# Unit 1's gelu moved ahead of unit 2's second centre tap, and half of the gate and residual of rows 0 to 3 moved into stage P3 of the down product

## The chip, the cores and the metric

The kernel runs on one core of one Trainium2 chip. A core has five engines that run their own instruction streams side by side: TensorE (PE in the profile; PEld is its weight load), VectorE (DVE), ScalarE (ACT), GpSimd (POOL) and SyncE (SP, which here only issues DMAs). Each stream runs in its written order, and an instruction that waits for another engine holds up everything behind it in its own stream. The metric is the time of one execution on the device in microseconds (us), lower is better.

## The reference

One block of a diffusion transformer on 1024 tokens of 1024 channels: token mixers, a layer norm, a feed-forward part with a 3x3 depthwise convolution, and a last layer norm. The change touches the feed-forward part and the last layer norm alone:

```
def conv_ffn(h, w_up, conv_w, conv_b, w_down, grid_rows):
    a, g = jnp.split(h @ w_up, 2, axis=-1)
    bsz, t, f = a.shape
    a = dwconv3x3(a.reshape(bsz, grid_rows, t // grid_rows, f), conv_w).reshape(bsz, t, f) + conv_b
    return (jax.nn.gelu(a, approximate=False) * g) @ w_down

# in reference(), with ALPHA = 2 ** 0.25 and mx[5] the gate of the second half
        ffn_x = conv_ffn(modulate(x_new, mx[3], mx[4]), ffn_up[l], ffn_conv_w[l], ffn_conv_b[l], ffn_down[l], rows)
        x_new = layer_norm(ALPHA * x_new + mx[5] * ffn_x, ln2_g[l], ln2_b[l])
```

All of it is computed in float32; the kernel splits each operand of a product into a high and a low part and multiplies three times.

## The kernel before

All engine calls go through one helper, so nearly every instruction carries line 57 in the profile, and groups are told apart by their tiles.

**The up product.** `ffn_up` works through 22 units of 128 hidden channels. Each unit is one Strassen-like product of seven partial products, numbered 1 to 7 in the code (a step such as "(3,2)" below is unit 3, product 2), of twelve 128x512 matmuls each. The convolved half of a unit collects in a pair of PSUM banks, `zv` (tile psA), of which there are two, so that unit 3's pair is the one that unit 1 gives back when its gelu has read it. The other half goes through single banks (tile psB). A unit's vector work is: `a` is formed on DVE for the two halves of the tokens, `centre(g, a)` puts the centre tap and bias into `zv` on ACT (tile psA from a, par), `conv` adds the other eight taps on DVE (eight SCALAR_TENSOR_TENSOR into psA), `gelu` reads `zv` on ACT into tile `h`, and `finish` multiplies `h` by the gate half on DVE. Weight halves are cut by `prepare(n)`: ACT casts the high part (tile wf), POOL subtracts to get the low part.

The first three units are started by hand (`u0`, `u1`, `u2` in `ffn_up`), with every engine's order written out; from unit 3 on a loop does the same in a fixed rhythm. In the hand-written part, `u1.conv()` runs on DVE while PE does (2,3), (1,4), (2,4) and (3,1). Then DVE forms u2's second `a`, ACT does u2's second centre tap, and DVE does `u1.finish` and `u2.conv()`. (3,2) opens unit 3's pair of banks; (3,3) adds to that pair's second bank, after ACT has copied `r` out of it and, on the pair's first bank, done unit 3's first centre tap.

**The down product.** `ffn_down` is one more such product of 1024x2816 by 2816x1024, of seven stages in the order 1, 2, 6, 5, 3, 7, 4 (called P1 and so on), with 11 forms (hidden slices) in each and 4 row tiles of 12 matmuls in all for each form. Accumulators X (stages 1, 6, 7, 4) and Y (2, 5, 3) are four PSUM banks each, one for each row tile of a half; the first two are tile psB, the others psA. Form i+4's high part is cast on ACT (`high`) and its low part subtracted on DVE (`low`, two instructions of 128x512 a form in P7 and P4: tiles fl and dw) at the start of iteration i. In stages 5, 7 and 4 the last 3, 3 and 5 forms are multiplied at the end, row tile by row tile, so that some row tiles are done earlier.

Outputs are eight row tiles (tile fy) of two column halves. Rows 0 to 3 get their first half from P1 and P2, their second half from P1, P6 (copied out of X at the start of P5) and P5, P3 (in Y). `out(t, c, bank, add)` gives the steps for row t, half c: `begin` adds the bank, `mid` fetches the residual input over the POOL queue (tile fx, three buffers) and multiplies by the gate row, `end` adds ALPHA times the residual and takes `bn_stats` of the half. `chain` makes mean and inverse deviation from those statistics, `last(t, c)` does the two layer-norm instructions on a half and sends it out. These steps stand in a list `todo`, from which each iteration takes one (two in the first five of P7) after its `low`, so they share DVE's one queue with the low parts that PE waits for. Rows 4 to 7 end with X after P7 (second half: `begin`, which must read X before P4 may add to it) and after P4 (first half), the latter as the program's tail: rows 6 and 7 first, then 4, then 5, each with its own `chain` and `last`.

Of the kernel before, what the change touches and what calls it, by code (L numbers as in the profile page):

```python
# [7 lines left out]
F32 = mybir.dt.float32  # L8
# [4 lines left out]
ALU = mybir.AluOpType  # L13
# [3 lines left out]
P = 128  # L17
T = 1024
D = 1024
# [6 lines left out]
ALPHA = 2.0 ** 0.25  # L26
# [41 lines left out]
class Builder:  # L68
# [1034 lines left out]
    def ffn_up(self, ys):  # L1103

        nc = self.nc
        tt = nc.vector.tensor_tensor
        us = [self.Unit(self, f) for f in range(FT)]
        u0, u1, u2 = us[:3]
        w11, w12, a0, g0 = self.first
        last = FT - 1  # L1110
# [96 lines left out]
        def go(u, k):  # L1207
            assert self.plan[self.at] == (u.f, k)
            bank = {6: u.x, 5: u.v, 7: u.x, 3: u.v, 4: u.x}[k]
            self.product(k, bank, self.forms.pop((u.f, k)), k == 5)  # L1210
            self.at += 1
# [41 lines left out]
        u1.conv()  # L1253
        go(u2, 3)
        tt(out=u2.a[:, 1], in0=u2.v, in1=u2.s[:, 1], op=ALU.add)
        u2.centre(1, u2.a[:, 1])
        self.prepare(self.at + 5)
        go(u1, 4)
        self.prepare(self.at + 5)
        u1.gelu()  # L1260
        go(u2, 4)
        self.prepare(self.at + 5)
        u1.finish((u1.x, u1.r[1]))
# [3 lines left out]
        for f in range(3, FT):  # L1267
# [8 lines left out]
            while self.at < len(self.plan) and self.plan[self.at][0] == f:  # L1276
                k = self.plan[self.at][1]
# [3 lines left out]
                if k == 7 and 4 <= f < 12:  # L1281
                    j = 36 + f
                    nc.vector.tensor_tensor_reduce(out=ada, in0=ada, in1=silc, scale=1.0, scalar=self.par[:, C_ADAB + j:C_ADAB + j + 1],
                                                   op0=ALU.mult, op1=ALU.add, accum_out=self.mods[:, j:j + 1])
# [157 lines left out]
    def ffn_down(self, dn):  # L1442
        nc, HF = self.nc, self.HF
        tt = nc.vector.tensor_tensor
# [24 lines left out]
        def load(i):  # L1469
            k, f = plan[i]  # L1470
            if k == 1 and f == 8:
                stores()
            if k == 1 and i < 3:
                return
            r = raws[i] = raw()
            h = {1: (0, 0), 2: (0, 1), 3: (0, 1), 4: (1, 1)}.get(k)
            src = self.h_part(*h, f) if h else self.s3[f][:, :] if k == 7 else self.s12[f][:, 1 if k == 6 else 0]
            nc.sync.dma_start(r[:, 0], src)
            if k == 1:
                nc.sync.dma_start(t1[f], self.w_part(0, 0, f))  # L1480
            w = {2: (1, 0), 3: (1, 1)}.get(k)
            if w:
                nc.sync.dma_start(r[:, 1], self.w_part(*w, f))
            if k == 3:
                exs[i] = self.Rt(nm="s2")
                nc.sync.dma_start(exs[i], self.s12[f][:, 1])

        def extra():
            return dn.tile([P, 2, 512], F32, tag="ex", bufs=3, name=self.name("ex"))
# [62 lines left out]
        ys, st = {}, {}  # L1552
        half = (slice(0, 512), slice(512, D))

        def new_y(t):
            if t not in ys:
                ys[t] = dn.tile([P, D], F32, tag="fy", bufs=8, name=self.name("fy"))
                st[t] = self.small([2, 6], nm="bnd", bufs=8)
            return ys[t]

        def out(t, c, bank, add):

            x, y = {}, new_y(t)[:, half[c]]

            def fetch():
                x[0] = dn.tile([P, 512], F32, tag="fx", bufs=3, name=self.name("fx"))
                nc.gpsimd.dma_start(x[0], self.xnew[t][:, half[c]])

            def begin():
                if add:  # L1570
                    tt(out=y, in0=y, in1=bank, op=ALU.add)
                else:
                    fetch()
                    tt(out=y, in0=bank, in1=gate[:, half[c]], op=ALU.mult)

            def mid():
                fetch()
                tt(out=y, in0=y, in1=gate[:, half[c]], op=ALU.mult)

            def end():  # L1580
                self.residual(x[0], y, st[t][:, c, :])
            if add:
                return begin, mid, end
            return begin, end
# [15 lines left out]

        def last(t, c):
            m, r = stat[t]
            y, s = ys[t][:, half[c]], half[c]
            nc.vector.scalar_tensor_tensor(out=y, in0=y, scalar=m, in1=lng[:, s], op0=ALU.subtract, op1=ALU.mult)
            nc.vector.scalar_tensor_tensor(out=y, in0=y, scalar=r, in1=lnb[:, s], op0=ALU.mult, op1=ALU.add)
            (nc.gpsimd if t < 4 else nc.sync).dma_start(self.out[t * P:(t + 1) * P, s], y)

        def both(*parts):
            def run():
                for p in parts:  # L1610
                    p()
            return run

        todo = []
        for i in range(LD):
            load(i)
        gate, lng, lnb = rows = [dn.tile([P, D], F32, name=n) for n in ("gate5", "ln2_g", "ln2_b")]
# [5 lines left out]
        for i in range(N):  # L1623
            k, f = plan[i]
            if i + LD < N:
                load(i + LD)
            if i < 3:

                nc.sync.dma_start(t1[i], self.w_part(0, 0, i))
            if i == 18:  # L1630
                nc.sync.dma_start(gate, self.gate5.broadcast_to([P, D]))
            if i in (20, 22):
                self.row(("ln2_g", "ln2_b")[(i - 20) // 2], rows[(i - 18) // 2])
            for l, _, at, by in sums:
                j = i - at + 3
                if j >= 0 and j % by == 0 and j // by < HF:
                    l(j // by)
            if i + LP + 1 < N:
                high(i + LP + 1)
            if i + LP < N:  # L1640
                low(i + LP)
            if i == 0:
                u = self.prev
                u.new = lambda shape, nm: extra()
                u.gelu()
                u.fetch()
                u.finish()
                for part in u.sums():
                    part()
            for _, g, at, by in sums:  # L1650
                j = i - at
                if j >= 0 and j % by == 0 and j // by < HF:
                    g(j // by)
            if i == first[2]:
                Y = [self.bank("B"), self.bank("B")]
                yp = self.pair()
                Y += [yp[:, 0], yp[:, 1]]
            n = group.get(k, 0)
            if f < HF - n:
                for t in range(4):  # L1660
                    multiply(i, t)
            elif f == HF - 1:
                if k == 4:
                    for g in todo:
                        g()
                    todo = []

                for part in ((2, 3), (0,), (1,)):
                    for t in part:
                        for j in range(i - n + 1, i + 1):  # L1670
                            multiply(j, t)
                    for t in part:
                        if k == 5:
                            nc.scalar.copy(new_y(4 + t)[:, half[1]], Y[t])
                        elif k == 7:
                            b, *e = out(4 + t, 1, X[t], True)
                            b()
                            todo += e
                        else:
                            for g in out(4 + t, 0, X[t], False):  # L1680
                                g()
                    if k == 4:
                        chain(*(4 + t for t in part))
                        for t in part:
                            for c in range(2):
                                last(4 + t, c)

            if f < 4:
                if k == 2:
                    nc.scalar.copy(new_y(f)[:, half[0]], X[f])  # L1690
                elif k == 5:
                    nc.scalar.copy(ys[f][:, half[1]], X[f])
            if f == 0 and k == 5:
                for x in zip(mids, ends):
                    todo += x
            if f == 0 and k in (6, 7):
                o = [out(t, 0 if k == 6 else 1, Y[t], True) for t in range(4)]
                todo += [x[0] for x in o]
                mids, ends = [x[1] for x in o], [x[2] for x in o]
                if k == 7:  # L1700
                    fin = [lambda t=t, c=c: last(t, c) for t in range(4) for c in range(2)]
                    todo += [mids[0], both(ends[0], mids[1]), both(ends[1], mids[2]), both(ends[2], mids[3]), both(ends[3]),
                             both(lambda: chain(0, 1, 2, 3), fin[0]), *fin[1:]]
            for _ in range(2 if k == 7 and f < 5 else 1):
                if todo:
                    todo.pop(0)()
# [47 lines left out]
```

## Time and profile before

| what | value |
|---|---|
| time, median of 3 runs | 1317.91 us (1316.45 to 1319.5) |
| the profiled execution's own time | 1315.14 us |
| its span, first to last instruction | 1313.4 us |
| mean granted TensorE clock | 0.99 |
| DVE busy | 1015.4 us |
| ACT busy | 550.9 us |
| POOL busy | 363.4 us |
| HBM read, written | 168.32 MB, 39.08 MB |

A profile row in order of time gives start, duration, engine, line, operation, output tile from input tiles, shape and count; a bracket at its end is the idle time of that engine just before, with the tile that released it. Start-to-start distances are shorter than durations where an engine overlaps one instruction's end with the next one's start. A row by stretch gives, for the stretch, its length, busy time and instructions of PE, PEld, DVE, ACT and POOL, then the granted TensorE clock (1.00 is full), the DMA share and GB/s. The seven stages of the down product follow each other from 1077 us; P3 stands at about 1198 to 1228 us, P7 at 1228 to 1258, P4 from 1261, and DVE works alone from where PE ends.

### The profile page before, as it was taken

The numbers are of one execution on the slowest core, as the hardware profiler recorded it, in microseconds if no ns is written. First come the engines' busy times: TensorE is split into PE (matmuls) and PEld (weight loads), VectorE is DVE, ScalarE is ACT, GpSimd is POOL, SyncE is SP. The second block draws the span as 40 slices with busy tenths as digits, with TensorE's granted clock in tenths as the row PEclk, the third lists the DMA queues.
The fourth block names the chain that finished last, engine by engine and source line by source line (L and its number), as shares of the span: only waits on it lengthen the run. The fifth ranks groups of instructions, "written<-read, shape, count | busy, mean of one in ns | idle before, by whom it ended". The sixth has DMA issues, their size and how long they took to land. (4 is left out here: it accounts for less than half of the span.)

```text
span 1313.4 us, 17643 instructions
## 1 busy us (share of the span) xinstructions
PE 1244.1 (95%) x6348; PEld 1044.6 (80%) x6348; DVE 1015.4 (77%) x1790; ACT 550.9 (42%) x980; POOL 363.4 (28%) x309
## 2 busy tenths in 40 slices
PE   4999999999999989999998999999999999999993
PEld 3887888889888878777876788888888888888872
DVE  7968984686949768697797777777766776988797
ACT  4836444443332241345363444444344443545420
POOL 0000000000000000000017788888988872000020
PEclk9999999999999999999999999999999999999997
DMA  9763234104123054346564434542443268999242
GB/s 332 265 198 124 96 121 152 49 24 159 54 71 113 17 178 144 124 167 206 172 188 135 172 117 159 177 136 89 160 145 124 101 228 306 352 312 363 88 145 89
DMA packets 99672, 208.56 MB, mean 159 GB/s; under 512 B 10224, under 2 KB 31360, under 8 KB 99584
## 3 DMA queue, kind: packets, MB, share of 16 engines
q1 hardware_dynamic: 94784, 190.65, 42.7%
q0 software_dynamic: 4800, 16.78, 3.5%
q8 instruction: 50, 0.82, 0.2%
q14 instruction: 38, 0.31, 0.1%
HBM read 168.32 MB, written 39.08 MB: 158 GB/s over the span
## 5 line engine op out<-in xcount | busy, mean ns | idle before, releaser
L57 DVE SCALAR_TENSOR_TENSOR psA<-a,par,psA 128x945 f32<-128x945 f32 (+2 forms) x176 | 215.9, 1227 | 21.6 <-ACT psA L57 16.2
L57 PE MATMUL psA<-x,wf 128*128 128x512 f32 x708 | 172.2, 392 | 6.4 <-ACT h L57 3.4
L57 PE MATMUL psB<-xk,wf 128*128 128x512 f32 x672 | 176.7, 390 | 0.9 <-ACT s L57 0.9
L57 PEld LDWEIGHTS psA<-x,wf 128*128 128x128 f32 x708 | 133.8, 189 | 35.8 <-ACT psA L57 3.9
L57 PEld LDWEIGHTS psB<-xk,wf 128*128 128x128 f32 x672 | 126.1, 188 | 27.7 <-ACT s L57 1.3
L57 POOL DMA_DIRECT2D wd<-pk x16 | 8.7, 542 | 500.7 <-ACT pk L57 463.0
L57 PE MATMUL psA<-xh,wh 128*128 128x512 f32 x320 | 126.8, 396 | 2.0 <-ACT wh L57 1.2
L57 POOL TENSOR_TENSOR wf<-raw,wf 128x512 fp32r<-128x512 f32 x95 | 123.1, 1301 | 20.0 <-ACT wf L57 19.4
L57 PE MATMUL psA<-xh,wl 128*128 128x512 f32 x320 | 126.1, 394 | 0.1
L57 PE MATMUL psA<-xl,wh 128*128 128x512 f32 x320 | 125.9, 393 | 0.0
L57 PE MATMUL psB<-x,wf 128*128 128x512 f32 x384 | 104.7, 389 | 0.0
L57 PEld LDWEIGHTS psB<-x,wf 128*128 128x128 f32 x384 | 72.0, 188 | 15.3 <-issue 0.2
L57 ACT CAST wh<-r 128x512 fp32r<-128x512 f32 x76 | 44.5, 619 | 84.7 <-PE psA L57 57.3
L57 ACT CAST wf<-raw 128x512 fp32r<-128x512 f32 x95 | 58.7, 618 | 47.5 <-PE psA L57 27.4
L57 DVE TENSOR_TENSOR a<-psA,s 128x512 f32<-128x512 f32 x39 | 27.0, 691 | 60.6 <-PE psA L57 59.0
L57 PEld LDWEIGHTS psA<-xh,wh 128*128 128x128 f32 x320 | 60.2, 188 | 14.1 <-ACT wh L57 1.6
L57 PEld LDWEIGHTS psA<-xh,wl 128*128 128x128 f32 x320 | 60.2, 188 | 12.4 <-DVE wl L57 0.5
L57 PEld LDWEIGHTS psA<-xl,wh 128*128 128x128 f32 x320 | 60.2, 188 | 11.7 <-issue 0.2
L57 DVE TENSOR_TENSOR kq<-kq,F 128x1024 f32<-128x1024 f32 x56 | 67.5, 1216 | 0.2
L57 DVE TENSOR_TENSOR wl<-r,wh 128x512 fp32r<-128x512 f32 x76 | 49.9, 687 | 22.4 <-PE psB L57 13.2
L57 ACT CAST fh<-dr 128x512 fp32r<-128x512 f32 (+1 forms) x47 | 36.1, 768 | 72.8 <-DMA dr<-in_w_down 22.2
L57 PE MATMUL psB<-kq,A 128*128 128x128 f32 x448 | 60.4, 289 | 0.8 <-ACT A L57 0.7
(365 smaller groups left out, 2928.9 us busy)
## 6 DMA issues: line engine op xcount, KB each, us to landing
raw<-in_wup SPq DMA_DIRECT2D x38, 512.0 KB, 5.5
ada<-in_ada SPq DMA_DIRECT2D x32, 512.0 KB, 4.4
r<-in_win SPq DMA_DIRECT2D x56, 256.0 KB, 2.8
ex<-in_w_down SPq DMA_DIRECT2D x55, 256.0 KB, 5.4
dr<-hd SPq DMA_DIRECT2D x44, 256.0 KB, 5.4
hd<-h SPq DMA_DIRECT2D x20, 512.0 KB, 3.0
dr<-s SPq DMA_DIRECT2D x33, 256.0 KB, 5.3
adat<-in_ada SPq DMA_DIRECT2D x16, 512.0 KB, 7.0
```

Of the source, the lines that this page charges most:

```text
L57: ins = f(*args, **kw)
```

## The change

It has two parts.

First, in the hand-written start of `ffn_up`, one `prepare` and `u1.gelu()` move from behind `u2.centre(1, ...)` to ahead of it; the number of instructions is the same.

Second, in `ffn_down`, the second column half of rows 0 to 3 is computed in another order. Before, all of it came in P7: add the bank, multiply by the gate, add ALPHA times the residual. Now `early` runs in P3's first four iterations: it multiplies the part that is already in the row tile (P1, P6) by the gate and adds ALPHA times the residual. In P7, `late` multiplies Y by the gate into a buffer of fx, and `late2` adds that to the row and takes the statistics. That is one instruction more for each of the four rows. With it, `last` takes a row's 1024 columns in one pair of instructions and one DMA, for all rows but row 5 (the last one), which keeps its halves.

```
-        self.prepare(self.at + 5)
+        self.prepare(self.at + 5)
+        u1.gelu()
         u2.centre(1, u2.a[:, 1])
         go(u1, 4)
         self.prepare(self.at + 5)
-        u1.gelu()
...
+            def early():
+                mid()
+                nc.vector.scalar_tensor_tensor(out=y, in0=x[0], scalar=ALPHA, in1=y, op0=ALU.mult, op1=ALU.add)
+            def late():
+                x[1] = dn.tile([P, 512], F32, tag="fx", bufs=3, name=self.name("fx"))
+                tt(out=x[1], in0=bank, in1=gate[:, half[c]], op=ALU.mult)
+            def late2():
+                tt(out=y, in0=y, in1=x[1], op=ALU.add)
+                nc.vector.bn_stats(out=st[t][:, c, :], in_=y)
+            if add == "early":
+                return early, late, late2
...
-            y, s = ys[t][:, half[c]], half[c]
+            s = slice(0, D) if c is None else half[c]
+            y = ys[t][:, s]
...
-                            for c in range(2):
+                            for c in range(2) if t == 1 else (None,):
                                 last(4 + t, c)
...
-            if f == 0 and k in (6, 7):
-                o = [out(t, 0 if k == 6 else 1, Y[t], True) for t in range(4)]
+            if f == 0 and k == 6:
+                o = [out(t, 0, Y[t], True) for t in range(4)]
...
+            if f == 0 and k == 3:
+                o = [out(t, 1, Y[t], "early") for t in range(4)]
+                todo += [x[0] for x in o]
+            if f == 0 and k == 7:
...
-                    fin = [lambda t=t, c=c: last(t, c) for t in range(4) for c in range(2)]
+                    fin = [lambda t=t: last(t, None) for t in range(4)]
```

On ACT, at the end of the three hand-written units (wf are casts of weight halves, h from psA is unit 1's gelu, psA from a and par is unit 2's second centre tap):

```order
 L57 CAST wf_6427<-s_6425 128x512
+L57 CAST wf_6454<-s_6423 128x512
+L57 ACTIVATE h_6457<-psA_5975 128x1024
 L57 ACTIVATE psA_6403<-a_6386,par 128x512
-L57 CAST wf_6455<-s_6423 128x512
-L57 CAST wf_6471<-raw_6291 128x512
-L57 ACTIVATE h_6474<-psA_5975 128x1024
+L57 CAST wf_6473<-raw_6291 128x512
 L57 CAST wf_6489<-raw_6290 128x512
```

The gelu stood three instructions behind the centre tap, with two casts between; now it stands directly ahead of it, and one of the casts ahead of both.

On DVE, in the first iterations of P3 (dr and dw are the operands and low parts of forms, fy a row tile, fx the fetched residual):

```order
 L57 TENSOR_TENSOR dr_10350<-dr_10350,s_10353 128x512
 L57 TENSOR_TENSOR dw_10380<-dr_10323,dw_10379 128x1024
+L57 TENSOR_TENSOR fy_9629<-fy_9629,gate_9334 128x512
+L57 SCALAR_TENSOR_TENSOR fy_9629<-fx_10458,fy_9629 128x512
 L57 TENSOR_TENSOR dr_10361<-dr_10361,s_10364 128x512
 L57 TENSOR_TENSOR dw_10442<-dr_10350,dw_10441 128x1024
 L57 TENSOR_TENSOR tk_9317<-ex_10366 128x512
+L57 TENSOR_TENSOR fy_9653<-fy_9653,gate_9334 128x512
+L57 SCALAR_TENSOR_TENSOR fy_9653<-fx_10485,fy_9653 128x512
```

Two instructions come in after the low part of each of the first four iterations.

On DVE, in the middle of P7, before the change (fy with ln_g and ln_b are the layer norm's two instructions for a half row; dw are the low parts of P7's forms 9 and 10):

```order
-L57 SCALAR_TENSOR_TENSOR fy_9629<-fy_9629,finmv_10792,ln_g 128x512
-L57 SCALAR_TENSOR_TENSOR fy_9629<-fy_9629,finrs_10794,ln_b 128x512
-L57 TENSOR_TENSOR dw_10773<-dr_10690,dw_10772 128x512
-L57 TENSOR_TENSOR dw_10773<-tv_9347,dw_10772 128x512
-L57 SCALAR_TENSOR_TENSOR fy_9629<-fy_9629,finmv_10792,ln_g 128x512
-L57 SCALAR_TENSOR_TENSOR fy_9629<-fy_9629,finrs_10794,ln_b 128x512
-L57 TENSOR_TENSOR dw_10812<-dr_10712,dw_10811 128x512
-L57 TENSOR_TENSOR dw_10812<-tv_9347,dw_10811 128x512
```

and with the change (fl_10780 is form 8's low part, dw_10806 form 9's, dw_10829 form 10's):

```order
+L57 SCALAR_TENSOR_TENSOR fy_9653<-fy_9653,finmv_10760,ln_g 128x1024
+L57 SCALAR_TENSOR_TENSOR fy_9653<-fy_9653,finrs_10762,ln_b 128x1024
+L57 SCALAR_TENSOR_TENSOR fy_9678<-fy_9678,finmv_10760,ln_g 128x1024
+L57 SCALAR_TENSOR_TENSOR fy_9678<-fy_9678,finrs_10762,ln_b 128x1024
+L57 TENSOR_TENSOR fl_10780<-dr_10684,fh_10779 128x512
+L57 TENSOR_TENSOR fl_10780<-tv_9347,fh_10779 128x512
+L57 SCALAR_TENSOR_TENSOR fy_9701<-fy_9701,finmv_10760,ln_g 128x1024
+L57 SCALAR_TENSOR_TENSOR fy_9701<-fy_9701,finrs_10762,ln_b 128x1024
+L57 TENSOR_TENSOR dw_10806<-dr_10710,dw_10805 128x512
+L57 TENSOR_TENSOR dw_10806<-tv_9347,dw_10805 128x512
+L57 TENSOR_TENSOR dw_10829<-dr_10738,dw_10828 128x512
+L57 TENSOR_TENSOR dw_10829<-tv_9347,dw_10828 128x512
```

Half rows alternated with low parts from form 9 on, and the last two half rows stood behind X's reads; now all four whole rows stand ahead of form 9's low part.

More of the change, by code (lines that the diff above doesn't have):

```diff
@@ L1695, in ffn_down @@
                     todo += x
-            if f == 0 and k in (6, 7):
-                o = [out(t, 0 if k == 6 else 1, Y[t], True) for t in range(4)]
+            if f == 0 and k == 6:
+                o = [out(t, 0, Y[t], True) for t in range(4)]
                 todo += [x[0] for x in o]
                 mids, ends = [x[1] for x in o], [x[2] for x in o]
-                if k == 7:
-                    fin = [lambda t=t, c=c: last(t, c) for t in range(4) for c in range(2)]
+            if f == 0 and k == 3:
+                o = [out(t, 1, Y[t], "early") for t in range(4)]
+                todo += [x[0] for x in o]
+            if f == 0 and k == 7:
+                if True:
+                    mids, ends = [x[1] for x in o], [x[2] for x in o]
+                    fin = [lambda t=t: last(t, None) for t in range(4)]
                     todo += [mids[0], both(ends[0], mids[1]), both(ends[1], mids[2]), both(ends[2], mids[3]), both(ends[3]),
```

## The prediction

> **What bounds the kernel now.** The busy times of the page come first, then the waits of TensorE over the whole span (columns: us in total, times, longest):
>
> ```profile
> PE 1244.1 (95%) x6348; PEld 1044.6 (80%) x6348; DVE 1015.4 (77%) x1790; ACT 550.9 (42%) x980; POOL 363.4 (28%) x309
> PE psA L57 <- ACT h L57: 3.4, 1, 3.4
> PE psA L57 <- ACT psA L57: 3.1, 2, 1.8
> PE psB L57 <- DVE fy L57: 2.9, 1, 2.9
> ```
>
> PE is the bound nearly everywhere: in the up and down products its matmuls stand back to back, so whatever lets PE through earlier at a wait carries to the end, and work on other engines counts only where PE waits for it or, at the end, where PE has stopped. The change touches three such places: the 3.4 us on a gelu, the 2.9 us on row tiles, and the tail in which DVE works alone. The order of time around the first place:
>
> ```profile
> 700.52 10.05 DVE L57 SCALAR_TENSOR_TENSOR psA<-a,par,psA 128x945 f32<-128x945 f32 x8
> 710.49 0.69 DVE L57 TENSOR_TENSOR a<-psB,s 128x512 f32<-128x512 f32 x1
> 711.27 0.78 ACT L57 ACTIVATE psA<-a,par 128x512 f32<-128x512 f32 x1 [6.89 <-DVE a L57]
> 713.01 1.01 ACT L57 ACTIVATE h<-psA 128x1024 f32<-128x1024 f32 x1
> 714.06 0.69 DVE L57 TENSOR_TENSOR h<-h,psB 128x512 f32<-128x512 f32 x1 [2.89 <-ACT h L57]
> 714.08 4.61 PE L57 MATMUL psA<-x,wf 128*128 128x512 f32 x12 [3.39 <-ACT h L57]
> 714.66 1.04 DVE L57 TENSOR_TENSOR h<-h,r 128x512 f32<-128x512 f32 x1
> 715.63 10.05 DVE L57 SCALAR_TENSOR_TENSOR psA<-a,par,psA 128x945 f32<-128x945 f32 x8
> 723.99 2.88 PE L57 MATMUL psB<-xk,wf 128*128 128x512 f32 x12
> 725.78 1.03 ACT L57 ACTIVATE h<-psA 128x1024 f32<-128x1024 f32 x1 [3.72 <-DVE psA L57]
> 727.83 0.78 ACT L57 ACTIVATE psA<-a,par 128x512 f32<-128x512 f32 x1
> 728.66 3.04 PE L57 MATMUL psA<-x,wf 128*128 128x512 f32 x12 [1.79 <-ACT psA L57]
> ```
>
> The reader is to see two waits of PE in one chain. (3,2) at 714.08 waits for unit 1's gelu; that gelu is ready when u1's conv ends on DVE at 700.52 + 10.05 = 710.57, but stands on ACT behind the centre tap of 711.27 and two casts. u1's finish and u2's conv on DVE come after it, u2's gelu (725.78) after those, and unit 3's first centre tap (727.83) after that, which lets (3,3) go at 728.66. One thing more is in the rows: (3,2) takes 4.61 us for twelve matmuls, (3,7) at 723.99 only 2.88. The stretches say why (the figure after POOL's is the granted clock):
>
> ```profile
> 715.00:716.00 1.00, 1.00 (x4) 0.71 (x4) 1.00 (x2) 0.81 (x2) 1.00 (x2) 0.50 0.00 0
> 718.00:719.00 1.00, 1.00 (x6) 0.79 (x6) 0.96 (x2) 0.23 (x1) 1.00 (x2) 1.00 0.05 18
> 1262.00:1263.00 1.00, 1.00 (x4) 0.75 (x3) 0.96 (x3) 0.00 (x0) 0.00 (x0) 0.50 0.00 0
> 1265.00:1266.00 1.00, 1.00 (x7) 0.81 (x6) 1.00 (x2) 0.00 (x0) 0.09 (x1) 1.00 0.89 311
> ```
>
> After the waits of 3.39 and 2.85 us the clock is 0.50 for some us; after the 1.79 us at 728.66, twelve matmuls take a normal 3.04. So a long wait costs twice: (3,2) lost 4.61 - 2.88 = 1.7 us more.
>
> **First part, the gelu.** What is queued ahead of the gelu afterwards is one cast, whose input POOL has had since 702, in time that ACT idles (6.89 us before 711.27). So the gelu starts at about 710.6 in place of 713.01 and (3,2) at 711.7 in place of 714.08; PE then has waited 1.0 us and keeps its clock. The centre tap now waits for the gelu (711.6 to 712.4) and finish starts at 711.7; u2's conv follows at 712.9 in place of 715.63, since the second multiply, 1.04 us at 714.66 while POOL was busy too, should take the usual 0.69 with POOL idle there (2.4 us earlier if not). I take 2.7, and the chain behind shifts with it: u2's gelu to 723.1, (3,3)'s release to 725.9. The casts that the gelu passed go at 712.3 and 712.8, several us ahead of the matmuls that need them.
>
> But PE reaches (3,3) earlier still: 2.4 from (3,2)'s start and 1.7 from the clock, so (3,7) ends at 726.87 - 4.1 = 722.8, and PE waits 725.9 - 722.8 = 3.1 us there in place of 1.79. That lies between the waits of 2.85 and 3.39 that dropped the clock. I take it that it drops again, for 1.6 us (1.5 and 1.7 at the two places). What is left is 2.7 - 1.6 = **1.1 us**; the bounds are 0.7 (2.4 - 1.7) and 2.7 (no drop).
>
> The Trainium skill, "TensorE: Matmul & The Clock Gate", section "Part 1: The HAM clock gate", has the clock halved after an idle window of about 3.4 us that runs freely, and its section on oscillation warns of gaps over 3.4 us only. By that reading a wait of 3.1 us would pass and the first part be worth 2.7; the row of 1261 disagrees, as 2.85 us sufficed there.
>
> **Second part, P3.** DVE gets eight instructions more there, of some 0.66 us: 5.3 us.
>
> ```profile
> 1196.00:1226.30 30.30, 30.30 (x134) 24.75 (x133) 20.03 (x27) 14.73 (x22) 0.00 (x0) 1.00 0.71 250
> fx<-xnew POOLq DMA_DIRECT2D x11, 256.0 KB, 3.1
> 1187.79 0.55 POOL L57 DMA_DIRECT2D fx<-xnew  x1 [5.52 <-DVE fy L57]
> ```
>
> DVE is idle 10.3 of these 30.3 us, and low parts are cut four forms ahead, which is over 10 us of PE, so this is hidden. The residuals come through three buffers; POOL has nothing else to do and fetched three of these four by 1187.79, the fourth follows when the first buffer is free and lands 3.1 us later, about two iterations ahead of its use. Were this cover gone, the 5.3 us would be PE's.
>
> **Second part, P7.** The rows of before:
>
> ```profile
> 1226.30:1261.00 34.70, 31.91 (x141) 26.09 (x139) 33.87 (x61) 15.88 (x29) 3.79 (x7) 1.00 0.40 129
> 1226.29 1.37 DVE L57 TENSOR_TENSOR fy<-fy,psB 128x512 f32<-128x512 f32 x2 [4.13 <-PE psB L57]
> 1231.18 0.69 DVE L57 TENSOR_TENSOR fy<-fy,gate 128x512 f32<-128x512 f32 x1
> 1231.90 0.69 DVE L57 SCALAR_TENSOR_TENSOR fy<-fx,fy 128x512 f32<-128x512 f32 x1
> 1232.63 0.69 DVE L57 BATCH_NORM_STATS2 bnd<-fy 128x6 f32<-128x512 f32 x1
> 1233.24 0.67 DVE L57 TENSOR_TENSOR fy<-fy,gate 128x512 f32<-128x512 f32 x1
> 1228.13 0.39 PE L57 MATMUL psB<-fh 128*128 128x512 f32 x1
> 1257.60 0.61 PE L57 MATMUL psB<-dw,dw 128*128 128x512 f32 x2
> 1259.04 1.28 DVE L57 TENSOR_TENSOR fy<-fy,psA 128x512 f32<-128x512 f32 x2
> 1261.06 0.77 PE L57 MATMUL psB<-dw 128*128 128x512 f32 x1 [2.85 <-DVE fy L57]
> 1265.31 0.39 PE L57 MATMUL psB<-fh 128*128 128x512 f32 x1
> ```
>
> DVE is busy 33.87 of 34.70 us here and sets when P4 may start: PE runs P7 from 1228.13 without a gap, ends by 1258.2, and waits until DVE has come to X's reads (1259.04 for rows 6 and 7, 1260.23 for the banks that P4 begins with). P4's first twelve matmuls then take 1265.31 - 1261.06 = 4.25 us at the half clock in place of 2.72: 1.5 us more.
>
> I set DVE's queue anew, from P3's end (0 = 1226.29). Distances by the rows: 0.72 to an instruction that needs the one before, 0.60 else. Late and late2 for four rows, 8.0 in place of 10.7 for begin, mid and end; `chain` 1.6 as before; low parts 2 x 0.60 for ten forms, 12.0. For the whole rows no 1024-wide form of this instruction is in the trace; its nearest rows are
>
> ```profile
> L57 DVE SCALAR_TENSOR_TENSOR psA<-a,par,psA 128x1008 f32<-128x1008 f32 x6 | 7.6, 1273 | 0.2
> 1291.48 0.75 DVE L57 SCALAR_TENSOR_TENSOR fy<-fy,finmv,ln_g 128x512 f32<-128x512 f32 x1
> 1292.27 0.75 DVE L57 SCALAR_TENSOR_TENSOR fy<-fy,finrs,ln_b 128x512 f32<-128x512 f32 x1
> 1292.94 0.74 DVE L57 SCALAR_TENSOR_TENSOR fy<-fy,finmv,ln_g 128x512 f32<-128x512 f32 x1
> 1285.90 0.69 DVE L57 TENSOR_TENSOR fy<-psA,gate 128x512 f32<-128x512 f32 x1 [3.35 <-PE psA L57]
> 1309.42 0.75 DVE L57 SCALAR_TENSOR_TENSOR fy<-fy,finrs,ln_b 128x512 f32<-128x512 f32 x1
> ```
>
> A half row takes 1.46 us (1291.48 to 1292.94), so 2.92 for two. By 1008 columns in 1.27 us, 1024 take 1.29, and a pair 2.53 with the same overlaps: 0.37 less a row. The bounds are no saving (2.92) and half (1.46); I take 2.53, as the row of 1008 is nearly the same width. Four rows are 10.1, all ahead of X's reads now, where six halves (8.7) stood before. Sum: 8.0 + 1.6 + 12.0 + 10.1 = 31.7, against the measured 1259.04 - 1226.29 = 32.75. X's banks for P4 are then read by 33.6, so P4 could start at 1259.9.
>
> The front of the queue is heavier, though. All rows stand ahead of form 9's low part, which DVE begins at 24.4 and ends at 25.7; PE, at 2.72 us a form from 1228.13 (1.84), needs it at 24.5. PE waits twice 0.7 us, for forms 9 and 10, too short for the clock, and ends P7 at 33.3 (1259.6) in place of 1258.1. That just fits under X's reads: P4 starts at 1259.9, 1.2 us earlier, at full clock, which gives 1.5 more: **2.7 us**. With bounds: 0 if whole rows save nothing (worked out below), 4.5 if PE waited nowhere.
>
> **The tail.** From 1285.90 to 1310.17 DVE works without a pause that the change touches. It starts 2.7 us earlier; rows 6, 7 and 4 save 0.37 each, **1.1 us** (0 to 4.4). Row 5 keeps its halves, so the last DMA is as before.
>
> **Sum.** 1.1 + 2.7 + 1.1 = 4.9 us: the profiled execution, 1315.14 us with a span of 1313.4, would go to 1310.2. The runs' median, 1317.91, is 2.8 above it; the same difference gives **1313.0 us**, 0.37% less.
>
> **The rivals.**
> - No clock drop at (3,3): 2.7 in place of 1.1, so 1311.4. For it: a wait of 1.79 passed, and two cases are few. Against it: 2.85 did not. Chance 0.25.
> - The first part's lead gets lost before the down product, since POOL is busy eight to nine tenths through the up product and cuts the low parts there: 3.8 us, 1314.1. Against it: POOL itself waits for casts that PE paces. Chance 0.08.
> - A whole row costs as much as its halves, 2.92: DVE comes to X's reads at 33.3 and P4 starts 0.4 us later than before; PE's waits for forms 9 and 10 grow to 1.5 us more, but in pieces, so the clock stays and 1.5 is gained. With the first part and no tail gain, 2.2 us: 1315.7, no measurable change. Chance 0.13.
> - Slower: in P3, DVE stalls on each of the four residuals. If each were fetched only when DVE stands at it, with 0.55 us of issue and 3.1 of landing, DVE would lose 14.6 us; with the 5.3 of work that is 19.9, of which the lead of four forms (4 x 2.72 = 10.9) covers half and 9 reach PE: 1313 + 9 = 1322. It decides from 3.3 us of stall a row, where what reaches PE passes the gain of 4.9 by 2.6. Against it: the fetches have the whole of P5. Chance 0.04.
>
> The forecast itself has 0.50.
>
> **How the numbers follow.** About 0.2% (2.6 us) is what a measurement of this kernel can tell from no change. The forecast at 4.9, no drop at 6.5 and lost lead at 3.8 lie beyond it and the fourth case does not; with some of the nearer cases falling short, faster 0.79, same 0.16, slower 0.05. The range takes in no drop with a further us of gain, below, and whole rows without saving, above: 1310.0 to 1316.0.
>
> **What would show it.** (3,2) released by 711.7 with the clock at full; (3,3) at about 726 after some 3.1 us, with 0.50 behind it (1.00 if the first rival holds). DVE out of P3 still idle ahead of 1226, PE without a wait in P3. In P7, two short waits of PE on dw low parts and none of 2.85 us on fy, P4 at full clock. 1024-wide rows at 1.29 us. Wrong would be: a long wait in P7's last forms with the clock at half, or DVE waiting for fx in P3.

## The result and the profile after

| | kernel before | changed kernel |
|---|---|---|
| first comparison: median of 4 runs | 1318.7 us (1316.45 to 1320.82) | 1309.42 us (1308.28 to 1310.44) |
| the profiled execution's own time | 1315.14 us | 1309.42 us |
| its span | 1313.4 us | 1307.7 us |
| ratio of the runs | | 0.993 [0.991, 0.9949] |

The changed kernel is faster, as forecast, but by more: its time lies 0.6 us below the range's lower end of 1310.0 and 3.6 us below the forecast of 1313.0. The two traces differ by less than the medians do, and the question of this section and the next is which of the two measures the change.

The page's busy times of the changed kernel, within 2.5 us those of before on every engine:

```profile
PE 1243.7 (95%) x6348; PEld 1043.0 (80%) x6348; DVE 1015.5 (78%) x1780; ACT 550.7 (42%) x980; POOL 360.9 (28%) x305
```

Its waits of TensorE over the whole span (us in total, times, longest), where the difference lies:

```profile
PE psA L57 <- ACT psA L57: 4.3, 2, 3.0
PE psA L57 <- ACT h L57: 1.1, 1, 1.1
```

Of the three waits that the prediction started from, the one for the gelu (h) is down from 3.4 to 1.1 us, the one for unit 3's centre tap (psA) has grown to 3.0, and the one for row tiles (fy, 2.9) is not in the list any more. The first place in order of time (start, duration, engine, line, operation, tiles, shape, idle time before):

```profile
709.15 1.02 ACT L57 ACTIVATE h<-psA 128x1024 f32<-128x1024 f32 x1 [5.78 <-DVE psA L57]
710.07 0.78 ACT L57 ACTIVATE psA<-a,par 128x512 f32<-128x512 f32 x1
710.23 3.02 PE L57 MATMUL psA<-x,wf 128*128 128x512 f32 x12 [1.06 <-ACT h L57]
711.41 10.06 DVE L57 SCALAR_TENSOR_TENSOR psA<-a,par,psA 128x945 f32<-128x945 f32 x8
721.57 1.02 ACT L57 ACTIVATE h<-psA 128x1024 f32<-128x1024 f32 x1 [4.98 <-DVE psA L57]
723.62 0.78 ACT L57 ACTIVATE psA<-a,par 128x512 f32<-128x512 f32 x1
724.45 4.38 PE L57 MATMUL psA<-x,wf 128*128 128x512 f32 x12 [3.05 <-ACT psA L57]
728.67 2.89 PE L57 MATMUL psB<-xk,wf 128*128 128x512 f32 x12
```

Three stretches behind the two waits, where the figure after POOL's is the granted clock:

```profile
715.00:716.00 1.00, 1.00 (x6) 0.84 (x5) 0.96 (x2) 0.00 (x0) 1.00 (x2) 1.00 0.99 274
724.50:725.50 1.00, 1.00 (x3) 0.81 (x4) 1.00 (x2) 0.96 (x2) 0.48 (x1) 0.50 0.00 0
726.00:727.00 1.00, 1.00 (x4) 0.81 (x3) 0.00 (x0) 0.00 (x0) 1.00 (x2) 0.50 1.12 397
```

The gelu goes ahead of the centre tap, (3,2) starts after 1.06 us of waiting at full clock (3.02 us for its twelve matmuls, 4.61 before), and the clock drop has moved to (3,3), which takes 4.38 in place of 3.04. The next product, (3,4), starts at 728.67; before the change it started 2.87 us later:

```profile
731.54 2.88 PE L57 MATMUL psB<-xk,wf 128*128 128x512 f32 x12
```

Of this 1.52 us were there already ahead of anything that the change touches (unit 0's gelu stands at 692.18 before and 690.66 after), so the first part brings 1.35 us.

The second part in order of time: the first early step in P3, DVE's wait at P3's end, and in P7 the first whole row, form 9's low part, the one listed wait of PE, the first reads of X and P4's first matmul:

```profile
1195.68 0.69 DVE L57 TENSOR_TENSOR fy<-fy,gate 128x512 f32<-128x512 f32 x1
1196.40 0.69 DVE L57 SCALAR_TENSOR_TENSOR fy<-fx,fy 128x512 f32<-128x512 f32 x1
1224.03 0.69 DVE L57 TENSOR_TENSOR fx<-psB,gate 128x512 f32<-128x512 f32 x1 [4.13 <-PE psB L57]
1235.96 1.28 DVE L57 SCALAR_TENSOR_TENSOR fy<-fy,finmv,ln_g 128x1024 f32<-128x1024 f32 x1
1248.43 0.69 DVE L57 TENSOR_TENSOR dw<-dr,dw 128x512 fp32r<-128x512 f32 x1
1249.17 1.10 PE L57 MATMUL psA<-dw,dw 128*128 128x512 f32 x2 [0.47 <-DVE dw L57]
1255.66 1.28 DVE L57 TENSOR_TENSOR fy<-fy,psA 128x512 f32<-128x512 f32 x2
1257.68 0.47 PE L57 MATMUL psB<-dw 128*128 128x512 f32 x1
```

P7 as one stretch, and a microsecond of P4, with the clock after POOL's figure:

```profile
1224.10:1257.60 33.50, 32.83 (x141) 25.89 (x139) 32.67 (x52) 11.76 (x21) 3.78 (x7) 1.00 0.44 148
1258.00:1259.00 1.00, 1.00 (x6) 0.70 (x5) 1.00 (x3) 1.00 (x3) 0.00 (x0) 1.00 0.91 344
```

DVE still idles 4.13 us at P3's end, to the hundredth as before, and no early step waits for its residual: the added work there is hidden. From S = 1224.03, the start of P7's vector work, the reads of X come at 31.63 (32.75 before), PE stops for no 2.85 us, and P4 runs at full clock. DVE's tail, and its last instruction:

```profile
1281.18 0.69 DVE L57 TENSOR_TENSOR fy<-psA,gate 128x512 f32<-128x512 f32 x1 [6.70 <-PE psA L57]
1303.54 0.75 DVE L57 SCALAR_TENSOR_TENSOR fy<-fy,finrs,ln_b 128x512 f32<-128x512 f32 x1
```

From S to the tail's start it is 57.15 us (59.61 before), 2.46 less; from there to the last instruction 22.36 (23.52), 1.16 less. The last instruction is 5.88 us earlier than before, and the parts add up: 1.52 at the program's start, which the change does not touch, 1.35, 2.46 and 1.16, less 0.61 lost between (3,4) and S. Most of that loss is one wait of PE in the first stage of the down product, for a low part (fl) that DVE cut late: an instruction ahead of it on DVE's queue had waited 6.54 us for a tile of weights (ex) to land.

```profile
1103.02 0.69 DVE L57 TENSOR_TENSOR tk<-ex,tk 128x512 f32<-128x512 f32 x1 [6.54 <-DMA ex<-in_w_down]
1105.97 0.50 PE L57 MATMUL psB<-fh,fl 128*128 128x512 f32 x1 [0.48 <-DVE fl L57]
```

Four kernels below that have the first part too (e1, e5, e6, e11) have no such wait in their traces, so it is not shown that the change causes it. Without it the trace gives the change about 5.0 us (1.35 + 2.46 + 1.16), while the medians of the first comparison differ by 9.3.

### The profile page after: what moved, and what is told of

It reads as the page before. It is cut to its first block, busy times and chain, and to the rows that moved or that the text cites. A ratio compares the mean times of both kernels' runs of the same rounds, so it can differ in the third digit from the quotient of the medians.

```text
span 1307.7 us, 17619 instructions
## 1 busy us (share of the span) xinstructions
PE 1243.7 (95%) x6348; PEld 1043.0 (80%) x6348; DVE 1015.5 (78%) x1780; ACT 550.7 (42%) x980; POOL 360.9 (28%) x305
```

## The experiments

Theory A holds that the change is worth the 5.0 us of the trace and that the rest is the level of the first runs of the kernel before. Theory B holds that all 9.3 are the change's. The kernels e1 to e4 were compared with 23 runs of the kernel before on the same chip, 1312.7 us median (1309.43 to 1316.92).

**e1, the gelu alone.** The kernel before with the first part:

```
+        self.prepare(self.at + 5)
+        u1.gelu()
         u2.centre(1, u2.a[:, 1])
-        self.prepare(self.at + 5)
...
-        u1.gelu()
```

> The first part alone: unit 1's gelu ahead of the centre tap, the down product as before. Theory A (what the two traces show, step by step): 1.3 us less than before (2.9 us from the chain, 1.5 us given back by the half clock behind the 3.05 us wait of (3,3)), ratio 0.999. Theory B (the medians' 9.3 us less are all the change's, and the trace of before shows too short a loss): this part or the other must bring some 4 us more than its rows say, so 1.3 to 5 us less, ratio 0.996 to 0.999. Under both, the trace shows (3,2) after a wait of 1.1 us at full clock and (3,3) after some 3 us at half.

Measured: 1312.33 us, ratio 0.9986 [0.9976, 0.9995], 1.8 us by the ratio. The trace has the changed kernel's two rows, and P4's wait of 2.85 us with the half clock behind it, as before the change. (3,2) and (3,3):

```profile
712.29 3.02 PE L57 MATMUL psA<-x,wf 128*128 128x512 f32 x12 [1.06 <-ACT h L57]
726.51 4.61 PE L57 MATMUL psA<-x,wf 128*128 128x512 f32 x12 [3.04 <-ACT psA L57]
```

**e2, the down product alone.** The kernel before with the second part, that is, the changed kernel with the lines of e1 put back.

> The second part alone: gate and residual in P3, whole rows, with unit 1's gelu where it was. Theory A: 2.5 us from P7 and 1.2 us from the tail, 3.6 us less, ratio 0.9973. Theory B: 3.6 to 8 us less, ratio 0.994 to 0.997. The trace should show (3,2) after 3.4 us at half clock, as before, and P4 at full clock.

Measured: 1309.05 us, ratio 0.9966 [0.9953, 0.9978], 4.5 us by the ratio. The rows of (3,2) and (3,3) are those of before; the tail starts at S + 57.13 and takes 22.37 us, as in the changed kernel:

```profile
710.69 4.62 PE L57 MATMUL psA<-x,wf 128*128 128x512 f32 x12 [3.39 <-ACT h L57]
725.29 3.02 PE L57 MATMUL psA<-x,wf 128*128 128x512 f32 x12 [1.79 <-ACT psA L57]
```

**e3 and e4, both kernels as they are.**

> The kernel before, once more, against itself: ratio 1.000 under both theories. Theory A: its single times spread over 4 us or more, and where two of its traces differ in time, they differ ahead of 690 us, where the change does nothing. Theory B: its times spread because the waits of PE at (3,2) and at P4, or the clock behind them, last longer in some executions.

> The changed kernel, once more, against before on the same chip. Theory A: 5.0 us less (1.3 + 2.5 + 1.2), ratio 0.9962. Theory B: 9.3 us less, ratio 0.993, as in the first comparison.

Measured: 1313.21 us for the kernel before, ratio to its other runs 1.0004 [0.9993, 1.0016], and 1308.78 us for the changed one, ratio 0.9957 [0.9945, 0.9969]. The interval holds theory A's 0.9962 and not B's 0.993. The changed kernel is 0.6 us from its first time; the kernel before is 5 to 6 us below its own. Their traces show that equal waits do not cost equally. (3,2) and P4's start in the kernel before (e3), in order of time:

```profile
712.37 5.49 PE L57 MATMUL psA<-x,wf 128*128 128x512 f32 x12 [3.39 <-ACT h L57]
...
1259.15 0.47 PE L57 MATMUL psB<-dw 128*128 128x512 f32 x1 [2.84 <-DVE fy L57]
```

Two stretches of e3 behind the second of these waits:

```profile
1260.00:1261.00 1.00, 1.00 (x6) 0.83 (x5) 0.96 (x3) 0.00 (x0) 0.00 (x0) 1.00 0.00 0
1262.00:1263.00 1.00, 1.00 (x6) 0.84 (x5) 0.96 (x3) 0.00 (x0) 0.00 (x0) 1.00 0.56 180
```

Here a wait of 2.84 us left the clock at full, where 2.85 halved it in the first trace, and (3,2) lost 2.6 us by the clock where it had lost 1.7. What (3,2) lost did not last: from unit 0's gelu to (3,4) it is 39.35 us here and 39.36 in the first trace. Of the 3.3 us between the two traces of this kernel (1311.81 and 1315.14), 1.7 lie ahead of unit 0's conv, as theory A expected, and 1.4 at P4's clock, as theory B did. In e4, (3,3) took 5.49 us after 3.03 of waiting. Taken step by step as above, e3 and e4 give the change 0.27, 1.02 and 1.16, together 2.45 us in place of 5.0, so the 5.0 of one pair of traces is itself uncertain by more than 2 us; the runs, of which there are more, give 5.6 with an interval from 4.1 to 7.2.

The next four kernels are the changed one with one thing different, beside 28 runs of the kernel before on the same chip, 1313.73 us median (1311.02 to 1318.62).

**e5, the clock kept at (3,3).** Twelve matmuls with a zero stationary operand (the expectation calls it the moving one) fill the wait; the zero tile is made at the start of `ffn_up` by one DVE instruction more, here and in e10, e11 and e13:

```
             self.product(k, bank, self.forms.pop((f, k)), start)
+            if (f, k) == (3, 7):
+                for j in range(12):
+                    nc.tensor.matmul(bank, self.zero, next(self.form("11", j % 4)), start=False, stop=j == 11, skip_group_check=True)
```

> The changed kernel with twelve matmuls more, of a zero moving operand, between unit 3's product 7 and product 3, where PE otherwise waits 3.04 us; the output is the same. Theory C (the wait at (3,3) ends by the gelu chain and costs once more by the clock that it halves): PE works in place of waiting, (3,3) is released at the same distance from (3,2) as before, its wait in the trace falls from 3.04 to about 0.3 us, its twelve matmuls take 2.9 to 3.0 us in place of 4.4 to 5.5, and the kernel is 1.4 to 2.5 us faster than the changed one: about 1307 where that is 1308.8, a ratio of about 0.9943 to the kernel before. Rival (the longer twelve matmuls come from something other than the clock, as competition with casts or low parts): they stay at 4.4 us or more, and the time stays within 0.5 us of the changed kernel's, or is up to 2.6 us longer, as (3,3) is pushed back by twelve matmuls.

Measured: 1306.95 us (1306.44 to 1307.51), ratio 0.9946 [0.9935, 0.9958]. The fillers and (3,3):

```profile
720.41 2.91 PE L57 MATMUL psB<-x,zero 128*128 128x512 f32 x12
723.61 3.02 PE L57 MATMUL psA<-x,wf 128*128 128x512 f32 x12 [0.29 <-ACT psA L57]
```

(3,3) starts 14.23 us behind (3,2), as in the changed kernel (14.22), and takes 3.02 instead of 4.38. So the chain through the gelu releases it, and the longer matmuls were the clock. Against the changed kernel of the comparison before, the ratio falls from 0.9957 to 0.9946, 1.4 us with overlapping intervals.

**e6, the layer norms of rows 1 to 3 later in P7.**

```
-                             both(lambda: chain(0, 1, 2, 3), fin[0]), *fin[1:]]
+                             both(lambda: chain(0, 1, 2, 3), fin[0]), *[both()] * 4, fin[1], *[both()] * 4, *fin[2:]]
```

> The changed kernel with the layer norms of rows 1 to 3 spread differently in P7: row 1 some iterations later and rows 2 and 3 behind the point at which DVE has read X for P4. Theory D (DVE's queue sets P4's start): with about 5 us less in it ahead of X's reads, P4 starts when PE has finished P7, about S + 31.9 us (S: DVE's first instruction behind the 4.13 us idle at P3's end), in place of about S + 33.6; the two waits of some 0.5 us for low parts in P7 vanish; about 1.8 us faster than the changed kernel. Rival (something else, as POOL's output DMAs or the casts, sets P4's start): P4 starts where it did and the time is the same within 0.5 us. The displaced rows come back as a wait if P4's first low parts get late behind them: then P4's PE waits for dw and the gain is smaller than 1 us.

Measured: 1309.78 us, ratio 0.9971 [0.9959, 0.9984]: no gain over the changed kernel. P4 did start at S + 31.76 (1255.52; S is 1223.76) in place of S + 33.65, with no wait in P7, but the tail started at S + 57.69, 0.54 later than in the changed kernel. The rows of P4 that say why, POOL's, DVE's and PE's:

```profile
1262.94 0.53 POOL L57 DMA_DIRECT2D out<-fy  x1 [3.19 <-DVE fy L57]
1263.46 1.64 POOL L57 DMA_DIRECT2D fx<-xnew  x3
1268.68 0.69 DVE L57 SCALAR_TENSOR_TENSOR fy<-fx,fy 128x512 f32<-128x512 f32 x1 [3.02 <-DMA fx<-xnew]
1275.08 0.50 PE L57 MATMUL psA<-fh,fl 128*128 128x512 f32 x1 [0.41 <-DVE fl L57]
1276.88 0.51 PE L57 MATMUL psA<-fh,fl 128*128 128x512 f32 x1 [0.47 <-DVE fl L57]
```

The output of row 3 stands on POOL's queue ahead of three residual fetches and waits there for the later layer norm; DVE waits 3.02 us for the fetched tile, the low parts behind it come late, and PE pays. From 1274.28 to 1281.25 PE did 21 matmuls, 4.8 us of work at 0.227 each, in 6.97 us. The 1.89 us gained at P4's start were more than given back, 2.2 of them here.

**e8, the early steps with half rows.** Gate and residual in P3, layer norms by halves everywhere:

```
-                            for c in range(2) if t == 1 else (None,):
+                            for c in range(2):
...
-                    fin = [lambda t=t: last(t, None) for t in range(4)]
+                    fin = [lambda t=t, c=c: last(t, c) for t in range(4) for c in range(2)]
```

> The changed kernel with the layer norms in half rows everywhere, as before the change; gate and residual still run in P3. Theory E (the second part works only as a whole, since half rows cost 1.46 us each and all eight now stand ahead of X's reads): DVE's queue is 8.0 + 1.6 + 12.0 + 11.7 = 33.3 us, P4 starts at about S + 35.2, 0.4 us later than before the change, PE waits about 3 us there, the tail takes as long as before, and only the first part's gain is left: ratio to before 0.9985 to 0.9995, 3.5 us slower than the changed kernel. Rival F (moving the gate and the residual is what pays, 2.5 us at P4): P4 at S + 33.6 and a ratio of about 0.997.

Measured: 1311.56 us, ratio 0.9977 [0.9964, 0.9989]; the interval holds theory E's upper figures and also 0.997. The trace decides between them: P4 at 1257.59, S + 35.18 against E's 35.2 and F's 33.6. (3,3) and P4's start in order of time:

```profile
724.27 3.02 PE L57 MATMUL psA<-x,wf 128*128 128x512 f32 x12 [3.04 <-ACT psA L57]
1257.59 0.47 PE L57 MATMUL psB<-dw 128*128 128x512 f32 x1 [2.99 <-DVE fy L57]
```

Two stretches of P4 in e8, with the clock after POOL's figure:

```profile
1258.00:1259.00 1.00, 1.00 (x6) 0.79 (x5) 1.00 (x3) 0.00 (x0) 0.00 (x0) 0.89 0.98 373
1259.50:1260.50 1.00, 1.00 (x3) 0.77 (x3) 0.96 (x3) 0.15 (x1) 0.00 (x0) 0.50 0.34 129
```

The tail starts at S + 60.23, 0.6 us later than before the change, and takes 23.51, as before. In this trace (3,3) kept its clock after 3.04 us, and P4 lost it after 2.99, about a microsecond into the matmuls.

**e9, whole rows without the early steps.** Gate and residual in P7 as before:

```
-            if f == 0 and k == 3:
-                o = [out(t, 1, Y[t], "early") for t in range(4)]
-                todo += [x[0] for x in o]
             if f == 0 and k == 7:
+                o = [out(t, 1, Y[t], True) for t in range(4)]
+                todo += [x[0] for x in o]
```

> The changed kernel with gate and residual of the second half of columns back in P7 as before the change, but the layer norms in whole rows. Theory E: DVE's queue is 10.7 + 1.6 + 12.0 + 10.1 = 34.4 us, P4 starts at about S + 36.4, 1.6 us later than before the change, after a wait of 4 us or more that halves the clock; the tail is 1.1 us shorter; with the first part's 1.2 a ratio to before of about 0.9993, 4 us slower than the changed kernel. Rival G (the saving of 0.37 us a row is what pays, in P7 as in the tail): P4 at S + 34 or earlier and a ratio of about 0.997.

Measured: 1313.57 us, ratio 1.0 [0.9989, 1.0011]. P4 starts at S + 36.12, after the longest wait of all; the tail starts 1.54 us later than before the change and is 1.15 shorter. P4's first matmul:

```profile
1259.24 0.52 PE L57 MATMUL psB<-dw 128*128 128x512 f32 x1 [4.20 <-ACT dw L57]
```

So by the traces the early steps alone lose 0.6 us, the whole rows alone lose 0.4, and together they gain 3.6 (2.46 + 1.16). Some 1.4 us of the 2.46 are the clock drop at P4, which the changed kernel does not have: the kernel before reaches the tail at S + 58.1 to 58.2 in e3 above and in e10 and e13 below, where that clock was kept.

The next three stood beside 17 runs of the kernel before on a second chip, 1314.09 us median (1311.97 to 1316.64).

**e10, the kernel before with its clock kept at (3,2) and P4.** Ten zero matmuls behind (3,1), and ten ahead of P4:

```
+            if (f, k) == (3, 1):
+                for j in range(10):
+                    nc.tensor.matmul(bank, self.zero, next(self.form("11", j % 4)), start=False, stop=j == 9, skip_group_check=True)
...
+            if k == 4 and f == 0:
+                for j in range(10):
+                    nc.tensor.matmul(Y[0], self.zero, forms[i][0][:, 1], start=j == 0, stop=j == 9, skip_group_check=True)
```

> The kernel before, with ten matmuls of a zero stationary operand behind unit 3's product 1 (where PE waits 3.39 us for the gelu) and ten ahead of P4 (where it waits 2.85 us); the output is the same and no wait of any other engine changes. Theory H (what differs from run to run of one kernel, and part of the level, is what the halved clock costs at these two waits): both waits shrink to about 1 us, the twelve matmuls behind each take 2.7 to 3.1 us, the kernel gets 1.5 to 3.5 us faster, ratio 0.997 to 0.999, and its runs lie within some 2 us of each other where those of the kernel before lie within 7. Rival J (the spread comes from elsewhere, such as the start of the program): about as much faster, but the runs lie as far apart as before's.

Measured: 1313.59 us (1312.08 to 1316.78), ratio 0.9996 [0.9987, 1.0006]. The expectation failed on the time and, with 4.7 us between the runs, on theory H's spread; rival J had the spread right. (3,2), (3,3) and P4's start in order of time:

```profile
711.05 3.02 PE L57 MATMUL psA<-x,wf 128*128 128x512 f32 x12 [1.10 <-ACT h L57]
725.66 4.45 PE L57 MATMUL psA<-x,wf 128*128 128x512 f32 x12 [3.43 <-ACT psA L57]
1259.39 0.50 PE L57 MATMUL psB<-dw 128*128 128x512 f32 x1 [0.46 <-DVE fy L57]
```

Both clocks were kept, and the tail started at S + 58.14, 1.5 us less than before. But (3,3) is released 14.61 us behind (3,2) whether the clock drops at (3,2) or not (14.58 before), so PE waited there for 3.43 us in place of 1.79, and the drop went to (3,3), where it is paid.

**e11, e5 and e6 together, with the later outputs on another queue.**

```
-            (nc.gpsimd if t < 4 else nc.sync).dma_start(self.out[t * P:(t + 1) * P, s], y)
+            (nc.gpsimd if t < 2 else nc.sync).dma_start(self.out[t * P:(t + 1) * P, s], y)
```

> The changed kernel with the twelve zero matmuls ahead of (3,3) of the run on the kept clock and the rows of the run on the later layer norms, where now the outputs of rows 2 and 3 go out over SP's queue and not POOL's. Theory K (the later rows gained 1.85 us at P4's start and lost 2.2 in P4, since on POOL's queue the residuals of rows 4 to 7 were fetched behind those two outputs, on which DVE stalled 3.02 us and made P4's low parts late): with the outputs elsewhere the residuals are fetched before 1255, no stall of DVE on fx, no wait of PE for low parts in P4; the tail starts at about S + 55.3 in place of 57.15; 1.8 us faster than the run on the kept clock, 3.3 us faster than the changed kernel, ratio to before 0.993. Rival L (DVE has no room for 5 us more work in P4, whatever the queue): PE waits for low parts in P4 again and the time is that of the run on the kept clock or 0.5 us more.

Measured: 1307.03 us (1303.95 to 1307.69), ratio 0.9947 [0.9934, 0.996]. In the trace theory K holds: POOL fetches the residuals 18 us earlier than in e6, counted from S, DVE waits for none, PE for no low part in P4, and the tail starts at S + 55.48 (S is 1220.35), 1.67 us less than in the changed kernel. The fetches and the tail's start:

```profile
1241.83 1.64 POOL L57 DMA_DIRECT2D fx<-xnew  x3
1275.83 0.69 DVE L57 TENSOR_TENSOR fy<-psA,gate 128x512 f32<-128x512 f32 x1 [1.55 <-PE psA L57]
```

The profiled execution is the one of 1303.95 us; the others lie between 1306.81 and 1307.69. The median is 1.5 us below e12's, not 3.3, and five runs do not settle how much of the trace's gain the runs hold.

**e12, the changed kernel a third time.**

> The changed kernel as it is, beside the two others of this call. Theory A (the change is worth 5 us): ratio to before 0.9955 to 0.9970. Theory B (it is worth 9): 0.993. Theory H also expects of it a spread between its runs smaller than before's, since one wait of 3 us is left in it of two.

Measured: 1308.48 us (1307.41 to 1310.72), ratio 0.996 [0.9948, 0.9972], as theory A has it. With e4, the change is worth 5.3 to 5.6 us.

**e13, the kernel before without any clock drop.** e10, with twelve more zero matmuls behind (3,7):

```
-            if (f, k) == (3, 1):
+            if (f, k) in ((3, 1), (3, 7)):
+                m = 10 if k == 1 else 12
```

> The kernel before, with the zero matmuls of the run before at (3,2) and at P4 and twelve more ahead of (3,3), where that run waited 3.43 us and its next twelve matmuls took 4.45. Theory H (the halved clock makes the spread from run to run, and a part of the level): no wait of PE over 1.5 us is left between 670 and 1280 us, the twelve matmuls of (3,3) take 3.0 us, 1.4 less; with P4's 1.45 the kernel is 3 us faster than before, ratio about 0.998, and its runs lie within 2 us. Rival J (the spread comes from the start of the program and other waits that no edit here touches): about as much faster, ratio 0.997 to 0.999, but the runs lie 4 to 5 us apart, as the starts of unit 0's conv do, 678.66 to 682.62 us in the traces so far. Rival M (what the first comparison's runs of the kernel before lost came from these drops): the runs of the kernel before beside it may then lie at 1318 again, and this kernel's stay at 1310.

Measured on a third chip, beside 17 runs of the kernel before of 1313.64 us median (1309.89 to 1316.74): 1311.94 us (1309.09 to 1315.01), ratio 0.9986 [0.9976, 0.9996]. That is 1.8 us by the ratio [0.5, 3.2], where 3 was expected: (3,3) is back at 3.06 us, but before it took 3.04, so only P4's 1.5 is a gain. The runs lie 5.9 us apart, so theory H falls: the clock drops are not what spreads the runs. Theory M found no support either, as the kernel before was at its usual level.

## Why the prediction was wrong

**The first part, right.** Forecast was (3,2) after 1.0 us at full clock, (3,3) after 3.1 us at half clock, and 1.1 us left; the trace has 1.06, 3.05 and 1.35, and e1 alone measured 1.8 [0.7, 3.2] us (its ratio's interval on 1312.7). The rival without a drop, given 0.25, is a real case: of the eight traces in which PE waits 3.03 to 3.43 us at (3,3), one kept the clock, e8. The Trainium skill, "TensorE: Matmul & The Clock Gate", section "Part 1: The HAM clock gate", has the clock follow a window of about 3.4 us that runs freely; that equal waits pass in one execution and cost 1.5 or 2.6 us in another fits it. Its figure as a threshold does not, since a wait of 2.85 us dropped the clock. The prediction's "a long wait costs twice" holds only where nothing behind it waits anyway: what (3,2) lost by the clock cost nothing before the change, since (3,3) was released 14.6 us behind (3,2) with the drop and without it (e10). Of the rival in which the lead is lost ahead of the down product, this trace has a part, the 0.61 us, by a late DMA and not by POOL.

**P3, right.** The work there is hidden, and the slower rival's stall on the residuals did not happen.

**P7 and P4, right.** Forecast: X's reads at S + 31.7, form 9's low part at 24.4, short waits of PE, full clock, 2.7 us. The trace has 31.63, 24.40 (1248.43), waits of 0.47 us and less, and 2.46. The rival with whole rows at the price of two halves has P4 start 0.4 us later than before the change; e8 bears that out (S + 35.18 against 34.77), and e9 shows the same of whole rows without the early steps (36.12). Neither half of this part works alone. One sentence in it was false: that no 1024-wide form of this instruction is in the trace of before. The list of its groups has one in another stage, at the duration that the change then showed:

```profile
L57 DVE SCALAR_TENSOR_TENSOR ly<-ly,mvt,ln_g 128x1024 f32<-128x1024 f32 x8 | 10.2, 1276 | 0.0
```

With this row the rival in which whole rows save nothing deserved almost none of its 0.13, and the range needed no such end. Luck had a share too: e3, the kernel before, kept its clock at P4 after a wait of 2.84 us, and against that trace this term is 1.02 us and not 2.46.

**The tail, right:** 1.1 us forecast, 1.16 measured.

**The step that failed is the last line of the sum:** "The runs' median, 1317.91, is 2.8 above it; the same difference gives 1313.0 us". The terms gave 4.9 us and 1310.2 us for the profiled execution, the trace 5.0 and 1309.42; the mechanisms were right, but that the sums agree to 0.1 us is partly luck, as e3 and e4 give 2.45. But the difference of 2.8 us belonged to those runs of the kernel before and not to the kernels: the changed kernel's median is its profiled time. The four runs of the first comparison lie at 1316.45 us or above, of the 85 that stood beside the experiments on three chips only 8 do, and their medians are 1312.7, 1313.73, 1314.09 and 1313.64. With the change at 5.0 us and a level of 1312.7 to 1314.1, the time is 1307.7 to 1309.1, and the changed kernel measured 1309.42, 1308.78 and 1308.48, the first 0.3 us above. The range failed with it: it held the bounds of every cost of the change, and none for the level on which the change was set.

Why those four runs took about 5 us longer stays open; the record does not name the chip they ran on. Only one execution of that time has a trace, the profiled one of 1315.14 us, and of its 3.3 us over e3's, 1.7 lie ahead of unit 0's gelu and 1.4 at P4's clock. e13 rules out that clock drops alone make the spread of the runs; it could not reach those four.

## What to carry to other kernels

A difference from one trace is set on the level of a few runs only with that level's own uncertainty in the range: each term of the change came out within 0.3 us of its first trace here, and the time was missed by 3.6. One pair of traces is not the change either: a second pair gave 2.45 us where the first gave 5.0. Where an engine waits at two places of one chain, shortening the first hands its gain to the second, with all that hangs on a long wait; count to the place where the chain ends, as with (3,3) here. And ahead of moving work behind the point at which it hurts, look at every queue that its DMAs stand in: in e6 an output that waited for its row cost all that the move had won.

## What the runs showed of the hardware

Of sixteen waits of TensorE between 2.84 and 4.20 us in these traces, at (3,2), (3,3) and P4's start, fourteen were followed by the half clock and two were not (3.04 us in e8, 2.84 in e3). What it cost, against 2.88 us for the twelve matmuls (2.72 in P4, start to start), was 1.5 to 1.7 us mostly, and 2.6 twice (5.49 us for twelve matmuls). In e8 P4's matmuls began at 1257.59; the clock's mean was still 0.89 from 1258 to 1259 us, and 0.50 from 1259.5 on: the drop can come after the wait is over.

The program's start varies by 4 us between kernels that are alike up to there (e2 and e1): unit 0's conv starts at 678.66 us in e2, at 679.02 in e11, at 682.09 in the first trace of the kernel before and at 682.62 in e1. Taken from there to DVE's last instruction, the kernel before takes 627.33 and 625.72 us (first trace, e3), and the changed kernel 622.97, 623.81 and 623.83 (first trace, e4, e12), which is 1.9 to 4.4 us less. Half of the 3.3 us between the two traces of the kernel before, and all of the 0.9 us between those of e4 and e12, were there already at unit 0's conv: a part of what looks like noise in single executions is over ahead of the stages that the change is in.
